# q and k turned into high and low parts, the attention scores as three part products, and one turn moved behind two score blocks

## The chip, the cores and the metric

The kernel runs on one core of a Trainium2 chip. The metric is the device time of one execution in microseconds (us): for the kernel before, the median of three runs. TensorE (PE) multiplies matrices out of the on-chip memory into eight accumulation banks of 128 x 512 fp32; PEld in the profile is its loading of the stationary operand. VectorE (DVE) and ScalarE (ACT) read the banks and do the elementwise work, and SyncE (SP) issues nearly all transfers.

## The reference, cut to what matters

One decoder layer on x of 256 x 1024 in fp32. Two attention branches of 8 heads of 64 work side by side on the same normalised input: "MoBA" (branch 0, with a rotary embedding on 16 of the 64 dimensions; at 256 positions there is one block, so it is causal attention) and "FoX" (branch 1, with a forget gate's cumulated logarithm added to the scores).

```python
h = rms_norm(x, attn_norm_g)
qa, ka, va, qb, kb, vb, f_logit, g_logit = split(h @ w_in)
qa, ka = partial_rope(rms_norm(qa, gq_a)), partial_rope(rms_norm(ka, gk_a))
qb, kb = rms_norm(qb, gq_b), rms_norm(kb, gk_b)
o_a = softmax(causal(qa @ ka.T / 8)) @ va                      # 8 heads
o_b = softmax(causal(qb @ kb.T / 8 + c[t] - c[s])) @ vb        # c = cumsum(log_sigmoid(f))
gates = sigmoid(g_logit + b_gate)
x = x + (gates[0] * (o_a @ w_moba) + gates[1] * (o_b @ w_fox)) @ w_out
u, g = split(rms_norm(x, ffn_norm_g) @ w_ffn_up)
x = x + (silu(conv3(g)) * u) @ w_ffn_down
```

## The kernel before, in words

All 256 positions stay on the chip; S = 256 is two tiles of P = 128 (NT = 2), and the 1024 features are KT = 8 slices. Weights stream through three raw buffers of 1 MB. Each half of such a buffer is split once: ACT rounds it into a high part (`whi`, L125, type fp32r), DVE subtracts that from the raw weights and leaves the low part (`wlo`, L126). There are six buffers of either, and `use` (L129) asks for the part five halves ahead of the one it hands out. The activations are split in the same manner (`xh`, `xl`). Every large product is then three products of parts, high x high, high x low and low x high, accumulated in one bank.

Not so the scores. `finish_qk` (L242) leaves normalised q or k of a branch in `qn`, positions on the partitions, as plain fp32. `turn_qk` (L271) transposes it on PE, block by block of 64 positions x 128 features (two heads) with an identity of 64 x 64: per branch 16 transposes for q and 16 for k, into two banks each; r says which half of the 64-row blocks and so which bank. ACT copies each of the four banks out, times the norm's gain, into `qT0`, `kT0`, `qT1`, `kT1` (L282), which hold two heads on 128 partitions: an even head on partitions 0 to 63, an odd one on 64 to 127. `scores(br, pair)` (L364) takes two heads: for each query tile t and head j one plain fp32 product (L374) of q's 128 positions with the first (t + 1) x 128 keys, 128 or 256 columns, out of 64 partitions; head j has a bank of its own. DVE then adds the mask or the bias and takes the row's extreme in one operation (L379, two per head: 128 and 256 columns), ACT takes the exponential and its sum (L382), DVE inverts (L384) and scales (L387). `turn` (L390) transposes the probabilities and `values` (L403) multiplies them by V. `gate` (L440) is a product of parts for the gates: of 256 columns, three per slice (L436 to L438), from a bank that DVE scales away (L443).

The order of PE's work is the program's order: it is written out by hand (`manual_schedule`, L48, and the list from L453 on). The order on ACT and DVE is made by a planner when the kernel is built; it can put an operation that is ready ahead of an earlier one that is not. The eight banks of the accumulation memory are handed out by one pool (`bank`, L53), so who gets a bank waits for the last reader of the one that had it. The part of PE's list around the change:

```python
    project(5, pv, 1)
    finish_v(pv, 1)
    forget_bias()
    turn_qk(qn, kn, 1)
    scores(0, 2)
    scores(0, 3)
    gate(0)
    gate(1)
    turn(0, 2)
```

Earlier on the list, `turn_qk(qn, kn, 0)` stands in the middle of projection 3, `scores(0, 0)` and `scores(0, 1)` in the middle of projection 4 and the four `scores(1, ...)` behind gates 1 and 3. Projections are L236 in the profile.

Two small tiles matter only as space: `sqs` (L543) and `rs2` (L568) of the second norm.

Of the kernel before, what the change touches and what calls it, by code (L numbers as in the profile page):

```python
# [8 lines left out]
F32 = mybir.dt.float32  # L9
F32R = mybir.dt.float32r  # L10
BF16 = mybir.dt.bfloat16
AF = mybir.ActivationFunctionType
ALU = mybir.AluOpType
# [4 lines left out]
P = 128  # L18
S = 256
NT = 2  # L20
D = 1024
KT = D // P
HD = 64
# [13 lines left out]
C_G2, C_BG, C_CW, C_CB, C_QG, C_BF, C_GR = 0, 8, 24, 90, 112, 116, 124  # L37
# [4 lines left out]
def decoder_block(ctx, tc, a, out):  # L42
    nc = tc.nc
# [6 lines left out]
    def T(shape, tag, bufs=1, dt=F32):  # L50
        return sb.tile(shape, dt, tag=tag, bufs=bufs, name=tag)

    def bank():  # L53
        return ps.tile([P, 512], F32, tag="bank", bufs=8, name="bank")
# [9 lines left out]
    for tag in ("xh", "xl"):  # L64
        T([P, KT, S], tag, 1, F32R)
    T([P, 2, KT, S], "pp", 1, F32R)
    for tag in ("qT0", "kT0", "qT1", "kT1"):
        T([P, 4, S], tag)

    nc.scalar.preload_act_table_set("natural_log_exp_and_others")  # L70

# [66 lines left out]
    def col(c, n=1):  # L138
        return sm[:, c:c + n]
# [59 lines left out]
    def apart(ap, b=2):  # L199
        return ap.rearrange("p (b t a) -> p b a t", b=b, a=2)  # L200

    def halves(ap):
        return ap.rearrange("p b (a t) -> p b a t", a=2)

    def halfrow(row, b=2):
        return row.rearrange("p (a t) -> p a t", a=2)[:, None].to_broadcast([P, b, 2, P])
# [35 lines left out]
    def finish_qk(pt, br, isk):  # L242

        qn = T([P, NT, NH, HD], "qn", 2)
        ss = T([P, NT, NH], "ss", 2)
        for t in range(NT):
            sq = T([P, W4], "sq", 2)
            nc.scalar.activation(sq, pt[t], AF.Square, scale=rs[:, t:t + 1])
            nc.vector.tensor_reduce(ss[:, t], sq.rearrange("p (h d) -> p h d", h=NH), axis=AX.X, op=ALU.add)
        f = T([P, NT, NH], "qf", 2)  # L250
        rsqrt_mean(f.rearrange("p t h -> p (t h)"), ss.rearrange("p t h -> p (t h)"), HD, [NT * NH], "qfv")
        for t in range(NT):
            nc.vector.tensor_scalar(f[:, t], f[:, t], rs[:, t:t + 1], 1.0 if isk else -HD ** -0.5, op0=ALU.mult, op1=ALU.mult)
            nc.vector.tensor_tensor(qn[:, t], pt[t].rearrange("p (h d) -> p h d", h=NH),
                                    f[:, t, :, None].to_broadcast([P, NH, HD]), op=ALU.mult)
        if br == 0:
            rc, rsn = rope[isk]
            p1 = T([P, NT, NH, 16], "p1", 1)
            p2 = T([P, NT, NH, 16], "p2", 1)
            x16 = qn[:, :, :, 0:16]  # L260
            nc.vector.tensor_tensor(p1, x16, rc[:, :, None, :].to_broadcast([P, NT, NH, 16]), op=ALU.mult)
            nc.vector.tensor_tensor(p2, x16, rsn[:, :, None, :].to_broadcast([P, NT, NH, 16]), op=ALU.mult)
            nc.vector.tensor_tensor(qn[:, :, :, 0:8], p1[:, :, :, 0:8], p2[:, :, :, 8:16], op=ALU.add)
            nc.vector.tensor_tensor(qn[:, :, :, 8:16], p1[:, :, :, 8:16], p2[:, :, :, 0:8], op=ALU.add)
        return qn


    turned = {}
    parts = [(slice(HD * r, HD * (r + 1)), ident[HD * r:HD * (r + 1), HD * r:HD * (r + 1)]) for r in range(2)]

    def turn_qk(qn, kn, br):  # L271

        for isk, (n, tag) in enumerate(((qn, "qT"), (kn, "kT"))):
            dst = T([P, 4, S], f"{tag}{br}")
            two = banks()
            for t in range(NT):
                for b in range(4):
                    c = slice((4 * t + b) * HD, (4 * t + b + 1) * HD)
                    for r, (rows, eye) in enumerate(parts):
                        nc.tensor.transpose(two[r][:, c], n[rows, t, 2 * b:2 * b + 2].rearrange("p h d -> p (h d)"), eye)  # L280
            for r in range(2):
                nc.scalar.activation(dst.rearrange("p b (t r c) -> p r t b c", t=NT, r=2)[:, r], two[r].rearrange("p (t b c) -> p t b c", t=NT, b=4),  # L282
                                     AF.Copy, scale=col(C_QG + 2 * br + isk))
            turned[br, isk] = dst


    bias = T([P, NH, 384], "bias")
# [64 lines left out]
    def forget_bias():  # L352

        tri_mask = mask3[:, None, 0:P].to_broadcast([P, NH, P])
        nc.vector.tensor_tensor(bias[:, :, 0:P], bias[:, :, P:2 * P], tri_mask, op=ALU.add)
        nc.vector.tensor_tensor(bias[:, :, 2 * P:3 * P], bias[:, :, 2 * P:3 * P], tri_mask, op=ALU.add)
# [7 lines left out]
    def scores(br, pair):  # L364
        s = T([P, 2, 384], "s", 3)
        nm = T([P, 2, 2], "nm", 4)
        l = T([P, 2, 2], "l", 4)
        sps = banks()
        for t in range(NT):
            for j in range(2):  # L370
                dst = sps[j][:, t * P:t * P + (t + 1) * P]
                ts, us = slice(t * P, (t + 1) * P), slice(0, (t + 1) * P)
                rows = parts[j][0]
                nc.tensor.matmul(dst, turned[br, 0][rows, pair, ts], turned[br, 1][rows, pair, us], start=True, stop=True)  # L374
        for j in range(2):
            h = 2 * pair + j
            sp = sps[j]
            for i, c in enumerate((slice(0, 128), slice(128, 384))):
                nc.vector.tensor_tensor_reduce(s[:, j, c], sp[:, c], mask3[:, c] if br == 0 else bias[:, h, c],  # L379
                                               scale=1.0, scalar=3e38, op0=ALU.add, op1=ALU.min, accum_out=nm[:, j, i:i + 1])  # L380
            for i, c in enumerate((slice(0, 128), slice(128, 384))):
                last_exp[:] = [nc.scalar.activation(s[:, j, c], s[:, j, c], AF.Exp, scale=-1.0, bias=nm[:, j, i:i + 1], accum_out=l[:, j, i:i + 1])]  # L382
        r = T([P, 2, 2], "r", 4)
        nc.vector.reciprocal(r, l)  # L384
        for j in range(2):
            for i, c in enumerate((slice(0, 128), slice(128, 384))):
                nc.vector.tensor_scalar_mul(s[:, j, c], s[:, j, c], r[:, j, i:i + 1])  # L387
        probs[br, pair] = s
# [29 lines left out]
    rsB = T([P, S], "rsB")  # L418
# [7 lines left out]
    def twin(kind, c, dst, mh, ml):  # L426

        for h in range(2):
            wh, wl = use((kind, c), h)
            for i in range(2):  # L430
                o = dst[:, i * S:(i + 1) * S]
                for k4 in range(4):
                    k = 4 * h + k4
                    w = slice(k4 * 256 + i * P, k4 * 256 + (i + 1) * P)
                    rh, rl = pairs(mh[:, k]), pairs(ml[:, k])
                    nc.tensor.matmul(o, wh[:, w], rh, start=(k == 0 and i == 0), stop=False)  # L436
                    nc.tensor.matmul(o, wh[:, w], rl, start=False, stop=False)  # L437
                    nc.tensor.matmul(o, wl[:, w], rh, start=False, stop=(k == KT - 1 and i == 1))  # L438

    def gate(c):  # L440
        gp = bank()
        twin("wg", c, gp, xh, xl)
        nc.vector.tensor_tensor(halves(gates[:, c]), apart(gp), halfrow(rsB), op=ALU.mult)  # L443
# [6 lines left out]
    def banks():  # L450
        return [bank() for _ in range(NT)]
# [6 lines left out]
    qn = finish_qk(pq, 0, 0)  # L458
# [3 lines left out]
    kn = finish_qk(pk, 0, 1)  # L462
# [4 lines left out]
    pq = banks()  # L467
    project(3, pq, 0)
    turn_qk(qn, kn, 0)
    project(3, pq, 1)  # L470
    forget_c()
    qn = finish_qk(pq, 1, 0)
    pk = banks()
    project(4, pk, 0)
    forget_d()
    scores(0, 0)
    scores(0, 1)
    project(4, pk, 1)
    kn = finish_qk(pk, 1, 1)
# [4 lines left out]
    project(5, pv, 1)  # L484
    finish_v(pv, 1)
    forget_bias()
    turn_qk(qn, kn, 1)
    scores(0, 2)
    scores(0, 3)
    gate(0)  # L490
    gate(1)
    turn(0, 2)
# [25 lines left out]
    for c in range(4):  # L518
# [11 lines left out]
        for j in range(2):  # L530
            b = 2 * c + j
# [8 lines left out]
    sq2 = T([P, 4, 2 * S], "V")  # L540
    acc = [bank() for _ in range(4)]
    x1 = xT
    sqs = T([P, S], "sqs")  # L543
    for c in range(4):
        for h in range(2):
            wh, wl = use(("wo", c), h)
            j = 2 * (c % 2) + h
# [8 lines left out]
            if c >= 2:  # L556
                xx = x1[:, 2 * j:2 * j + 2]
                nc.vector.tensor_tensor(halves(xx), apart(acc[j]), halves(xx), op=ALU.add)
                for b in (2 * j, 2 * j + 1):
                    g = col(C_G2 + b)  # L560
# [4 lines left out]
    for dst, src in ((0, 1), (2, 3), (0, 2)):  # L565
        nc.vector.tensor_tensor(sq2[:, dst], sq2[:, dst], sq2[:, src], op=ALU.add)
    nc.vector.tensor_tensor(sqs, sq2[:, 0, 0:S], sq2[:, 0, S:2 * S], op=ALU.add)
    rs2 = T([P, S], "rs2")  # L568

    def norm2():  # L570
        sp = bank()
# [153 lines left out]
```

## Time and profile before

| What | Value |
|---|---|
| Median of three runs | 356.55 us (356.46 to 356.7) |
| The profiled execution | 357.34 us, of which the span from the first to the last instruction is 355.5 us |
| Mean granted clock of TensorE | 0.999 |
| HBM read and written | 66.60 MB and 1.06 MB, 190 GB/s over the span |
| Loading from HBM, share of 16 engines | 51.7% |

A row of the chain or of a timeline starts with its start in us from the span's start and its length in us; then come the engine, the line of the kernel, and what is written from what. A row of groups has the count behind an x, then the busy time in us, the mean duration of one in ns, and the idle time of the engine just before, with what ended it. A plain fp32 product that the program issues once appears as two matmul records.

### The profile page before, as it was taken

What the parts mean: (1) busy time and instruction counts of PE and PEld (TensorE: products, weight loads), DVE (VectorE), ACT (ScalarE), POOL (GpSimd) and SP (SyncE); (2) the same over time, 40 slices, a digit from 0 to 9 for tenths busy, and PEclk for the clock granted to TensorE, in tenths of its full rate; (3) what the DMA queues carried; (4) which work ended last, traced back from release to release, by engine and by line L of the source; (5) the groups of instructions that cost most, each with busy time, mean ns of one, the idle gap of its engine ahead of it and who ended that gap; (6) DMA issues with size and microseconds to landing.
All of it is one profiled execution on the core that took longest, in us unless ns stands there. A gap on an engine that the chain in (4) does not pass through costs nothing.

```text
span 355.5 us, 6596 instructions
## 1 busy us (share of the span) xinstructions
PE 350.4 (99%) x2620; PEld 324.3 (91%) x2620; DVE 285.5 (80%) x534; ACT 228.8 (64%) x406; POOL 0.4 (0%) x6
## 2 busy tenths in 40 slices
PE   8999999999999999999999999999999999999995
PEld 4888888889899999999999999999999999999995
DVE  4989969888867756994997998897878788797953
ACT  5967576678849873553878866665756656666620
POOL 0000000000000000000000000000000000000000
PEclk9999999999999999999999999999999999999999
DMA  7986663663624453545644358655645646554003
GB/s 259 410 336 237 221 255 130 227 237 120 238 92 147 133 225 118 202 166 227 229 144 187 153 165 295 211 193 206 236 162 194 238 166 205 223 189 167 2 0 118
DMA packets 12558, 68.07 MB, mean 191 GB/s; under 512 B 1512, under 2 KB 3696, under 8 KB 5104
## 3 DMA queue, kind: packets, MB, share of 16 engines
q1 hardware_dynamic: 11328, 66.60, 51.7%
q10 hardware_dynamic: 1200, 1.06, 1.0%
q8 instruction: 20, 0.33, 0.4%
q14 instruction: 10, 0.08, 0.1%
HBM read 66.60 MB, written 1.06 MB: 190 GB/s over the span
## 4 chain that ended last, share of the span: by engine, by line
PE 98%; ACT 1%; DVE 0%; issue 0%
PE bank L590 22%; PE bank L236 18%; PE bank L591 11%; PE bank L641 6%; PE bank L640 6%; PE bank L639 5%; PE bank L436 4%; PE bank L438 4%; PE bank L437 4%; PE bank L527 2%; PE bank L555 2%; PE bank L554 2%; PE bank L529 2%; PE bank L528 2%; PE bank L553 2%; PE bank L411 2%
## 5 line engine op out<-in xcount | busy, mean ns | idle before, releaser
L126 DVE TENSOR_TENSOR wlo<-raw,whi 128x1024 fp32r<-128x1024 f32 x118 | 144.0, 1222 | 38.2 <-ACT whi L125 37.2
L125 ACT ACTIVATE whi<-raw 128x1024 fp32r<-128x1024 f32 x118 | 123.7, 1054 | 66.5 <-PE bank L590 20.7
L590 PE MATMUL bank<-pp,whi 128*128 128x512 f32 x352 | 116.2, 383 | 0.0
L591 PE MATMUL bank<-pp,wlo 128*128 128x256 f32 x352 | 95.9, 273 | 0.0
L590 PEld LDWEIGHTS bank<-pp,whi 128*128 128x128 f32 x352 | 66.6, 189 | 9.2
L591 PEld LDWEIGHTS bank<-pp,wlo 128*128 128x128 f32 x352 | 67.6, 192 | 0.0
L436 PE MATMUL bank<-xh,whi 128*128 128x256 f32 x128 | 35.6, 278 | 0.1
L437 PE MATMUL bank<-xl,whi 128*128 128x256 f32 x128 | 35.2, 275 | 0.0
L438 PE MATMUL bank<-xh,wlo 128*128 128x256 f32 x128 | 35.2, 275 | 0.0
L639 PE MATMUL bank<-qT,whi 128*128 128x256 f32 x112 | 30.8, 275 | 0.0
L640 PE MATMUL bank<-qT,whi 128*128 128x256 f32 x112 | 30.8, 275 | 0.0
L641 PE MATMUL bank<-qT,wlo 128*128 128x256 f32 x112 | 30.8, 275 | 0.0
L236 PE MATMUL bank<-whi,xh 128*128 128x512 f32 x96 | 29.8, 393 | 0.0
L236 PE MATMUL bank<-wlo,xh 128*128 128x512 f32 x96 | 29.1, 385 | 0.0
L236 PE MATMUL bank<-whi,xl 128*128 128x512 f32 x96 | 28.7, 380 | 0.0
L436 PEld LDWEIGHTS bank<-xh,whi 128*128 128x128 f32 x128 | 24.6, 192 | 1.1 <-ACT qT L282 0.5
L438 PEld LDWEIGHTS bank<-xh,wlo 128*128 128x128 f32 x128 | 24.6, 192 | 0.0
L437 PEld LDWEIGHTS bank<-xl,whi 128*128 128x128 f32 x128 | 24.6, 192 | 0.0
L639 PEld LDWEIGHTS bank<-qT,whi 128*128 128x128 f32 x112 | 21.5, 192 | 0.2
L640 PEld LDWEIGHTS bank<-qT,whi 128*128 128x128 f32 x112 | 21.5, 192 | 0.0
L641 PEld LDWEIGHTS bank<-qT,wlo 128*128 128x128 f32 x112 | 21.5, 192 | 0.0
L236 PEld LDWEIGHTS bank<-wlo,xh 128*128 128x128 f32 x96 | 18.3, 192 | 3.1 <-DVE wlo L103 0.6
(158 smaller groups left out, 644.7 us busy)
## 6 DMA issues: line engine op xcount, KB each, us to landing
raw<-in_wu SPq DMA_DIRECT2D x22, 1024.0 KB, 4.8
raw<-in_wd SPq DMA_DIRECT2D x11, 1024.0 KB, 4.8
raw<-in_qkv SPq DMA_DIRECT2D x9, 1024.0 KB, 5.0
raw<-in_wg SPq DMA_DIRECT2D x8, 1024.0 KB, 4.9
raw<-in_wb SPq DMA_DIRECT2D x4, 1024.0 KB, 5.2
raw<-in_wo SPq DMA_DIRECT2D x4, 1024.0 KB, 4.8
lead<-in_lead SPq DMA_DIRECT2D x8, 384.0 KB, 6.6
raw<-in_qkv SPq DMA_DIRECT2D x2, 512.0 KB, 8.0
```

Source lines behind the costliest of these rows:

```text
L125: whi = nc.scalar.activation(hi, raw, AF.Copy)
L126: nc.vector.tensor_tensor(lo, raw, hi.bitcast(F32), op=ALU.subtract)
L236: nc.tensor.matmul(pt[t], lhs[:, k, t * P:(t + 1) * P], rhs, start=(k == 0 and i == 0), stop=(k == KT - 1 and i == 2))
L411: nc.tensor.matmul(op[o:o + HD, n * S + i * P:(n + 1) * S], V[:, i, vc:vc + HD], pT[:, j, c], start=(i == 0), stop=(i == 1))
L436: nc.tensor.matmul(o, wh[:, w], rh, start=(k == 0 and i == 0), stop=False)
L437: nc.tensor.matmul(o, wh[:, w], rl, start=False, stop=False)
L438: nc.tensor.matmul(o, wl[:, w], rh, start=False, stop=(k == KT - 1 and i == 1))
L590: nc.tensor.matmul(two[i], wh[:, w], both, start=(k == 0), stop=False)
L591: nc.tensor.matmul(two[i][:, 0:S], wl[:, w], high, start=False, stop=(k == KT - 1))
L639: nc.tensor.matmul(o, wh[:, w], ah, start=first, stop=False)
L640: nc.tensor.matmul(o, wh[:, w], al, start=False, stop=False)
L641: nc.tensor.matmul(o, wl[:, w], ah, start=False, stop=end)
```

## The change

`turn_qk` leaves q and k as a high part (ACT, rounded to fp32r, times the gain) and a low part (DVE, the bank times the gain minus the high part); the low tiles `qL` and `kL` serve both branches in turn, and the tiles' inner order becomes tile by tile of positions (t, then pair, then 128 positions). Each of the four products of a `scores` call becomes three products of parts in fp32r, issued in the order of query tile, product, head. `turn_qk(qn, kn, 1)` moves behind `scores(0, 3)`. The space for the two new tiles comes from two small ones: `sqs` lies in a free part of `sq2`, and `rs2` takes the place of `rsB`.

```diff
-    for tag in ("qT0", "kT0", "qT1", "kT1"):
-        T([P, 4, S], tag)
+    for tag in ("qT0", "kT0", "qT1", "kT1", "qL", "kL"):
+        T([P, 4, S], tag, 1, F32R)
...
         for isk, (n, tag) in enumerate(((qn, "qT"), (kn, "kT"))):
-            dst = T([P, 4, S], f"{tag}{br}")
+            hi = T([P, NT, 4, P], f"{tag}{br}", 1, F32R)
+            lo = T([P, NT, 4, P], tag[0] + "L", 1, F32R)
             two = banks()
...
             for r in range(2):
-                nc.scalar.activation(dst.rearrange("p b (t r c) -> p r t b c", t=NT, r=2)[:, r], two[r].rearrange("p (t b c) -> p t b c", t=NT, b=4),
-                                     AF.Copy, scale=col(C_QG + 2 * br + isk))
-            turned[br, isk] = dst
+                h, l = (x.rearrange("p t b (r c) -> p r (t b) c", r=2)[:, r] for x in (hi, lo))
+                src = two[r].rearrange("p (n c) -> p n c", c=HD)
+                g = col(C_QG + 2 * br + isk)
+                nc.scalar.activation(h, src, AF.Copy, scale=g)
+                nc.vector.scalar_tensor_tensor(l, src, g, h.bitcast(F32), op0=ALU.mult, op1=ALU.subtract)
+            turned[br, isk] = hi, lo
...
         sps = banks()
+        todo = {}
         for t in range(NT):
             for j in range(2):
                 dst = sps[j][:, t * P:t * P + (t + 1) * P]
-                ts, us = slice(t * P, (t + 1) * P), slice(0, (t + 1) * P)
                 rows = parts[j][0]
-                nc.tensor.matmul(dst, turned[br, 0][rows, pair, ts], turned[br, 1][rows, pair, us], start=True, stop=True)
+                (qh, ql), (kh, kl) = turned[br, 0], turned[br, 1]
+                for i, (lhs, rhs) in enumerate(((qh, kh), (qh, kl), (ql, kh))):
+                    todo[t, i, j] = (dst.rearrange("p (u c) -> p u c", c=P), lhs[rows, t, pair], rhs[rows, 0:t + 1, pair])
+        for t, i, j in sorted(todo):
+            nc.tensor.matmul(*todo[t, i, j], start=(i == 0), stop=(i == 2))
...
-    turn_qk(qn, kn, 1)
     scores(0, 2)
     scores(0, 3)
+    turn_qk(qn, kn, 1)
     gate(0)
...
-    sqs = T([P, S], "sqs")
+    sqs = sq2[:, 1, 0:S]
...
-    rs2 = T([P, S], "rs2")
+    rs2 = T([P, S], "rsB")
```

## The prediction

> **What bounds the kernel now.** I read the page's busy table first, then the chain that ended last.
>
> ```profile
> span 355.5 us, 6596 instructions
> ...
> PE 350.4 (99%) x2620; PEld 324.3 (91%) x2620; DVE 285.5 (80%) x534; ACT 228.8 (64%) x406; POOL 0.4 (0%) x6
> ...
> PE 98%; ACT 1%; DVE 0%; issue 0%
> ```
>
> TensorE (PE) is busy for 99% of the span and is 98% of the chain; VectorE (DVE) and ScalarE (ACT) matter only where PE waits for them. So the question is what the change does to PE's own time around the scores, and whether it makes or ends a wait. The chain in order of time, its longest pieces, shows the scores (L374) and the one piece in these stages that is not PE:
>
> ```profile
> 58.22 1.51 PE bank L374 x16
> ...
> 76.38 1.27 ACT V L240 x2
> 77.65 0.94 ACT whi L125
> 78.59 0.59 ACT qT L282
> 79.22 0.38 PE bank L436
> ...
> 91.10 1.37 PE bank L374 x16
> ...
> 107.02 1.37 PE bank L374 x16
> ```
>
> Each row is a block of two calls of `scores`; the fourth lies between 76 and 79 us, where the chain leaves PE: gate 0 (L436) starts at 79.22, when ACT's first copy of q's turned bank (L282) ends. PE's timeline there:
>
> ```profile
> 75.96 0.59 PE L236 MATMUL bank<-whi,xl 128*128 128x512 f32 x2
> 76.49 1.22 PE L280 MATMUL bank<-cst,qn 64*128 64x64 f32 x32
> 77.55 1.53 PE L374 MATMUL bank<-kT,qT 64*128 64x128 f32 x16
> 79.22 0.38 PE L436 MATMUL bank<-xh,whi 128*128 128x256 f32 x1
> 79.44 0.28 PE L437 MATMUL bank<-xl,whi 128*128 128x256 f32 x1
> 79.55 0.28 PE L438 MATMUL bank<-xh,wlo 128*128 128x256 f32 x1
> 79.66 0.28 PE L436 MATMUL bank<-xh,whi 128*128 128x256 f32 x1
> ```
>
> **The price of a score.** Durations of matmuls overlap, so I use the distance from start to start.
>
> ```profile
> L374 PE MATMUL bank<-kT,qT 64*128 64x256 f32 x32 | 4.8, 377 | 0.0
> L374 PE MATMUL bank<-kT,qT 64*128 64x128 f32 x32 | 3.4, 288 | 0.0
> L280 PE MATMUL bank<-cst,qn 64*128 64x64 f32 x64 | 2.4, 226 | 0.0
> L345 PE MATMUL bank<-cst,cc 128*8 128x128 f32 x2 | 0.4, 273 | 0.0
> L236 PE MATMUL bank<-whi,xl 128*128 128x512 f32 x96 | 28.7, 380 | 0.0
> ...
> 57.84 0.38 PE L345 MATMUL bank<-cst,cc 128*8 128x128 f32 x2
> ```
>
> L345 is one plain fp32 product (a transpose by identity on all 128 rows, with only 8 weight columns): it is two records whose starts lie 0.38 − 0.273 = 0.107 us apart for 128 columns. L236 is a product of high and low parts: two products of 512 columns start 0.59 − 0.38 = 0.21 us apart (75.96 above), one record each. So a column costs 0.41 ns in the part format, and a plain fp32 product passes its columns twice in each of two records: four passes against one. That is what the change hopes to use: three single passes for four.
>
> But the heads already run side by side. Per call of `scores` there are 64 / 8 = 8 records, four of 128 columns (0.107 us each) and four of 256 (0.214 us). One after another that is 1.28 us per call, 2.57 us for two; the block takes 1.37 us. So the two heads, on rows 0 to 63 and 64 to 127, share the time: 2 x 0.107 + 2 x 0.214 = 0.64 us per call, 1.28 us per block, and the other 0.09 us is the entry and the exit. "Side by side" adds nothing.
>
> And the new form is held by weight loads. The loads (PEld):
>
> ```profile
> L436 PEld LDWEIGHTS bank<-xh,whi 128*128 128x128 f32 x128 | 24.6, 192 | 1.1 <-ACT qT L282 0.5 <-ACT pT L400 0.3 <-issue 0.2
> L374 PEld LDWEIGHTS bank<-kT,qT 64*128 64x128 f32 x64 | 4.5, 188 | 0.4 <-issue 0.2
> L280 PEld LDWEIGHTS bank<-cst,qn 64*128 64x128 f32 x64 | 2.2, 140 | 0.7 <-issue 0.7
> L345 PEld LDWEIGHTS bank<-cst,cc 128*8 128x8 f32 x2 | 0.2, 86 | 0.2
> ```
>
> 8 columns take 86 ns and 128 columns 188 ns: 102 ns for 120 columns, 0.85 ns a column, so 128 columns occupy the load path for 0.109 us, and the part format is no quicker (192). Every product loads its weights again, even the same ones (L436 and L437 both use whi). Of a chain of such products each step then takes the larger of its passes and a load: with 256 columns 0.105 against 0.109, seen as 0.11 between 79.44, 79.55 and 79.66; with 128 columns 0.053 against 0.109. After the change a call is six steps (three products by two query tiles) of two heads at a time. The low price of a step is 0.111 us, as L436 to L438 show. The high one is 0.115: in the transposes of L280 two heads' steps are (1.22 − 0.226) / 15 = 0.066 us apart, while their load occupies about 0.109 − (0.188 − 0.140) = 0.061, so a pair adds 0.005 to its load. A call thus goes from 0.64 us (0.65 with the step of 0.109 that a load sets on the narrow ones) to 6 x 0.111 = 0.67 or 6 x 0.115 = 0.69. The narrow tile loses what the wide one gains. Over eight calls that is (0.02 to 0.04) x 8 = +0.15 to +0.3 us; I take +0.2, nearer the upper row because the transposes are pairs too.
>
> The Trainium skill, "TensorE: Matmul & The Clock Gate", section "Back-to-back issue gap", gives about 81 ns for a 128-column product in a stream of load and product. By it, as an estimate, the three narrow steps of a call would take 0.243 us and the eight calls 0.7 us less than I forecast. The same page's Part 3 says that a load overlaps a running matmul only in another row group; by that the six steps would each pay load and passes in turn. The trace contradicts this second rule: products on all rows step at 0.11 us (79.44 to 79.66), no more than a load.
>
> **The moved turn.** Before, from the end of the last projection (75.96 + 2 x 0.215 = 76.39) to gate 0 at 79.22 are 2.83 us: turn, two calls, and the wait for ACT. After, the two calls come first, and they need only q and k of the first branch, long turned; the turn follows, without a DMA in it, passing two calls on PE's hand-written order and, on ACT and DVE, whatever the planner puts there. PE then has: change to 64 rows 0.10 (76.39 to 76.49), first exposed load 0.10, twelve steps of 0.111 to 0.115 = 1.33 to 1.38, sixteen transposed pairs at 0.066 = 1.05, change back 0.10: 2.68 to 2.73, gate 0 at 79.07 to 79.12. That is 0.10 to 0.15 us sooner, the scores' extra included. Before, gate 0 had the first of the turn's banks, as its wait for L282 shows; the banks come round in turn, the two calls and the turn have changed places, and so I expect gate 0 in the first bank of the first moved `scores`. So its wait is no more ACT's copy but DVE's reductions of that bank:
>
> ```profile
> 76.51 1.21 DVE L126 TENSOR_TENSOR wlo<-raw,whi 128x1024 fp32r<-128x1024 f32 x1
> 78.62 1.22 DVE L126 TENSOR_TENSOR wlo<-raw,whi 128x1024 fp32r<-128x1024 f32 x1 [0.91 <-ACT whi L125]
> 79.77 0.28 DVE L379 CUSTOM_DVE_ANT_0 s<-bank,cst 128x128 f32<-128x128 f32 x1
> ...
> 80.32 0.29 DVE L379 CUSTOM_DVE_ANT_0 s<-bank,cst 128x128 f32<-128x128 f32 x1
> ```
>
> The first call's scores are complete at about 76.6 + 0.68 = 77.3; DVE is in a wlo until 77.72 and then idle for 0.91. The reductions of one bank take 80.32 − 79.77 = 0.55 (the 128 and the 256 columns), so the bank is free at about 78.3, 0.8 us before PE wants it. What is late next is then PE itself.
>
> **DVE's new work.** Four subtractions per turn, eight in all, each 128x512 out of a bank:
>
> ```profile
> L254 DVE TENSOR_TENSOR qn<-bank,qf 128x512 f32<-128x512 f32 x4 | 2.6, 681 | 0.0
> ...
> 50.69 1.23 DVE L126 TENSOR_TENSOR wlo<-raw,whi 128x1024 fp32r<-128x1024 f32 x1 [1.78 <-ACT whi L125]
> ...
> 52.58 0.68 PE L236 MATMUL bank<-whi,xh 128*128 128x512 f32 x2
> ...
> 82.88 1.01 DVE L387 TENSOR_SCALAR s<-s,r 128x128 f32<-128x128 f32 x4
> ...
> 90.14 0.96 PE L398 MATMUL bank<-cst,s 64*128 64x64 f32 x24
> ```
>
> At 0.68 us (L254's row, an operation of the same size out of a bank) that is 2.7 us a turn, 5.4 us in all, counted at nothing. In the first turn the idle 1.78 us ahead of 50.69 and the rest up to 52.6 hide it; a turn's bank now comes free only after ACT's copy and DVE's subtraction, and the next projection may want one at 52.58. In the second the cover is longer: the probabilities that PE turns at 90.14 are scaled from 82.88, so 83.9 + 2.7 = 86.6 still leaves 3.5 us. If the cover were gone, PE would wait for the part that sticks out, up to 1 us in the first turn. ACT's copies keep their size. The removed tiles (sqs inside sq2, rs2 in rsB's place) add no instruction, and their first uses stay in the order of the same engine; nothing for them.
>
> **The sum.** Second block with its turn −0.10 to −0.15; the three other blocks 3 x 2 x (0.02 to 0.04) = +0.1 to +0.2; DVE 0. Together −0.05 to +0.1, about nothing. The profiled execution took 357.34 us, 0.8 above the median of the three timed runs, 356.55; on the median I forecast 356.5. A difference of 0.2%, 0.7 us, is about what can be told from none.
>
> **The rivals.** *Narrow products are not held by the load.* If the 128-column steps ran at the transposes' 0.066 us, a call would be 3 x 0.066 + 3 x 0.113 = 0.54 us, and eight calls 8 x (0.68 − 0.54) = 1.1 us below my sum: 355.4. For it: transposed pairs do run at 0.066. Against: their load is the short one (140 ns), the scores' is 188. The skill's 81 ns would lie between.
>
> *DVE holds gate 0's bank* (the other side). Its place is 76.5 to 80 us: if the planner again puts the second wlo ahead of the reductions, as it did at 78.62, they start at 79.77 and the bank is free at 80.32; gate 0 starts 80.4 rather than 79.1: 356.5 + 1.3 = 357.8. It decides from the point where DVE begins that bank after 78.5. For it: that very order in the trace. Against: there the scores came 1 us later than they will now, and the whi that this wlo needs is ready only at 78.59.
>
> *Narrow part products take the slow form.* The trace has no product of parts below 256 columns. If these ran as plain fp32, two records of two passes, a narrow step would be 0.214 and a call 3 x 0.214 + 3 x 0.113 = 0.98: +0.3 x 8 = 2.4 us, 358.9. Against: all the products of parts that are shown, of 256 and of 512 columns, pass each column once, and no row shows a format that changes its passes with the width. If the heads fell apart into twelve steps, a call would be 1.36 us and the time 362; against it stand the fp32 blocks, which share.
>
> **How the numbers follow.** My forecast 0.62, all of it within 0.2%. Narrow products fast 0.16, of which nearly all falls below 0.2%, with a little from the wait at gate 0 that ends. DVE at gate 0 0.10, the slow form 0.06, heads apart 0.02, another wait of DVE's 0.04; of these some of the last stays within 0.2%. So faster 0.17, same 0.62, slower 0.21. The forecast's own range is 356.2 to 356.9; the range that leaves out the slow form and the split heads runs from the fast narrow products, 355.3, to DVE at gate 0, 357.8.
>
> **What would show it.** Right: L374 has 96 records of one pass; two-call blocks of 1.39 to 1.47 us in the chain in place of 1.37; starts of narrow and wide steps alike 0.11 apart; L436 after the moved turn at about 79.1 with no ACT piece before it; DVE 5.4 us busier with no PE wait on it. Wrong: blocks near 1.1 us (narrow steps at 0.066), blocks near 2 us, or a DVE piece ahead of gate 0.

## The result, and the profile after

The changed kernel takes 360.66 us (median of 4 runs, 360.51 to 360.72) against 356.6 us (356.46 to 356.7) for the kernel before on the same chip: ratio 1.011, 95% interval 1.0095 to 1.0125. It is 4 us slower, where 356.5 was forecast and 357.8 was the end of the range. The profiled execution took 360.51 us with a granted clock of 0.995.

The page after, the lines that answer to those of before:

```profile
span 358.7 us, 6674 instructions
...
PE 352.3 (98%) x2652; PEld 326.2 (91%) x2652; DVE 290.3 (81%) x542; ACT 229.4 (64%) x406; POOL 0.4 (0%) x6
...
PE 95%; DMA 2%; DVE 1%; ACT 0%; issue 0%; DVEq 0%
```

PE is no longer 98% of the chain: 2% is a transfer and 1% DVE. DVE is 4.8 us busier (290.3 − 285.5) by the eight subtractions: e9 below, which has the three products without them, shows 285.4. The chain after, in order of time:

```profile
58.62 1.23 DVE wlo L126
60.09 0.35 ACT s L390
60.44 8.52 DMA bias<-cd
68.98 1.23 DVE bias L359
...
71.32 0.29 DVE s L395
71.75 0.97 PE bank L406 x12
72.71 7.06 PE bank L236 x24
79.78 1.57 PE bank L382 x24
81.35 1.00 PE bank L281 x32
82.35 0.31 PE bank L444
...
94.16 1.43 PE bank L382 x24
...
110.15 1.44 PE bank L382 x20
```

Read from below: the two last blocks of scores (L382) are 1.43 and 1.44 us, and gate 0 (L444) follows the moved turn (L281) with no ACT piece between them, both as forecast. But from 58.6 to 72.7 us the chain leaves PE. The 1 MB transfer of the forget gate's bias lands at 68.98, DVE's addition (L359) waits for it, the scaling of the second pair's probabilities (L395) stands behind that addition in DVE's queue, and PE waits for the scaling with `turn(0, 1)` (L406). None of these instructions is one that the change touches. PE's table of waits after has one row for these stages (us in total, times, the longest):

```profile
PE bank L406 <- DVE s L395: 1.4, 1, 1.4
```

DVE itself waits 5.77 us for the bias, as its timeline in the next section shows; before it was 1.76.

Where PE's time went, from the start of a step's first matmul to the start of the next step's in PE's timeline, in us (each to within 0.01):

| Step | before | after | e1 (below) |
|---|---|---|---|
| scores(0,0), (0,1) | 1.51 | 1.57 | 1.57 |
| turn(0,0), (0,1) | 0.89 | 2.88 | 0.89 |
| second half of projection 5 | 5.38 | 7.06 | 5.38 |
| q's and k's second turn with scores(0,2), (0,3) | 2.73 | 2.58 | 2.58 |
| turn(0,2), (0,3), scores(1,0), (1,1) | 2.26 | 2.32 | 2.32 |
| turn(1,0), (1,1), scores(1,2), (1,3) | 2.26 | 2.33 | 2.32 |
| sum | 15.03 | 18.74 | 15.06 |

The sum grows by 3.71 us; the spans differ by 358.7 − 355.5 = 3.2, since the first score began 0.52 us sooner in the profiled execution after (57.63 against 58.15). Of the 3.71 us, 1.99 + 1.68 are in two steps that the diff doesn't touch, 0.04 in those that it does.

### The profile page after: what moved, and what is told of

It reads as the page before. It is cut to its first block, busy times and chain, and to the rows that moved or that the text cites. A ratio compares the mean times of both kernels' runs of the same rounds, so it can differ in the third digit from the quotient of the medians.

```text
span 358.7 us, 6674 instructions
## 1 busy us (share of the span) xinstructions
PE 352.3 (98%) x2652; PEld 326.2 (91%) x2652; DVE 290.3 (81%) x542; ACT 229.4 (64%) x406; POOL 0.4 (0%) x6
## 4 chain that ended last, share of the span: by engine, by line
PE 95%; DMA 2%; DVE 1%; ACT 0%; issue 0%; DVEq 0%
PE bank L598 21%; PE bank L236 15%; PE bank L599 11%; PE bank L649 5%; PE bank L647 5%; PE bank L648 5%; PE bank L444 4%; PE bank L446 4%; PE bank L445 4%; DMA bias<-cd 2%; PE bank L535 2%; PE bank L562 2%; PE bank L561 2%; PE bank L536 2%; PE bank L563 2%; PE bank L537 2%
## 5 line engine op out<-in xcount | busy, mean ns | idle before, releaser
L444 PE MATMUL bank<-xh,whi 128*128 128x256 f32 x128 | 35.6, 278 | 0.0
L444 PEld LDWEIGHTS bank<-xh,whi 128*128 128x128 f32 x128 | 24.6, 192 | 0.4 <-issue 0.2
```

## Where the late bias comes from

DVE's timeline before and after, from the first scores on (start, length; the idle time before an operation and its releaser in brackets):

```profile
59.11 0.29 DVE L379 CUSTOM_DVE_ANT_0 s<-bank,cst 128x128 f32<-128x128 f32 x1
...
61.60 1.19 DVE L126 TENSOR_TENSOR wlo<-raw,whi 128x1024 fp32r<-128x1024 f32 x1
...
65.47 1.23 DVE L355 TENSOR_TENSOR bias<-bias,cst 128x1024 f32<-128x1024 f32 x1 [1.76 <-DMA bias<-cd]
...
67.81 1.00 DVE L387 TENSOR_SCALAR s<-s,r 128x128 f32<-128x128 f32 x4
```

```profile
58.62 1.23 DVE L126 TENSOR_TENSOR wlo<-raw,whi 128x1024 fp32r<-128x1024 f32 x1
59.76 0.28 DVE L387 CUSTOM_DVE_ANT_0 s<-bank,cst 128x128 f32<-128x128 f32 x1
...
68.98 1.23 DVE L359 TENSOR_TENSOR bias<-bias,cst 128x1024 f32<-128x1024 f32 x1 [5.77 <-DMA bias<-cd]
...
70.21 1.20 DVE L360 TENSOR_TENSOR bias<-bias,cst 128x1024 f32<-128x1024 f32 x1
71.32 1.00 DVE L395 TENSOR_SCALAR s<-s,r 128x128 f32<-128x128 f32 x4
```

The planner has put one `wlo`, that of weight half 23, ahead of the score reductions, at 58.62 instead of 61.60: 3.0 us sooner in the two profiles, 2.5 us sooner when each is counted from its first score (58.15 and 57.63). The planner also moved the second addition ahead of the scalings, from 73.48 to 70.21. The early `wlo` frees a raw buffer as much sooner, and SP, whose queue holds nothing but the next weight transfer, issues it at once. First SP's timeline, before and after (the row covers two issues; the second ends with the row), then the table of DMA issues, before for the bias alone and after for what was issued from 59.4 us on (the last number is the us from issue to landing):

```profile
55.48 7.70 SPq L121 DMA_DIRECT2D raw<-in_wg  x2
```

```profile
54.97 5.23 SPq L121 DMA_DIRECT2D raw<-in_wg  x2
```

```profile
bias<-cd ACTq DMA_DIRECT2D x1, 1024.0 KB, 5.0
```

```profile
raw<-in_wg SPq DMA_DIRECT2D x1, 1024.0 KB, 4.9
bias<-cd ACTq DMA_DIRECT2D x1, 1024.0 KB, 8.5
```

Before, the second weight issue ends at 55.48 + 7.70 = 63.18, well after the bias transfer was issued (65.4 − 5.0 = 60.4). After, it ends at 60.20, just ahead of the bias, which is issued at 60.44: two transfers of 1 MB are under way together. The weights, issued first by 0.57 us (59.87), take 4.9 us as they do alone, and the bias takes 8.5 us in place of 5.0.

The early `wlo` also holds up the issue of the bias. In ACT's queue an exponential (L390) stands between the issue of cd, the small transfer that the bias is read from, and that of the bias. It waits for DVE's first reduction, and that now stands behind the `wlo`. ACT's timeline after:

```profile
58.52 0.53 ACTq L353 DMA_DIRECT2D cd<-pT  x1
60.09 0.40 ACT L390 ACTIVATE s<-s,nm 128x128 f32<-128x128 f32 x1 [1.50 <-DVE nm L387]
60.44 0.40 ACTq L354 DMA_DIRECT2D bias<-cd  x1
```

The bias is issued 1.92 us behind cd; before it was 1.39 (59.04 to 60.43), and in e2 below, whose `wlo` is back in its place, 1.33. Without these 0.5 us the bias would have been issued at about 59.9, at the same moment as the weights. No run separates this delay from the earlier weight transfer.

The theory (Q in the expectations, where other letters stand for rivals): an early `wlo` starts a weight transfer next to the bias transfer; the bias is late, and in DVE's queue the scalings that PE waits for stand behind it. Three rivals: the new products or subtractions cost the time themselves; DVE's order alone, the additions ahead of the scalings, does it without the transfer; the halved clock that follows PE's wait makes most of it.

## The experiments

Each is compared with the kernel before on the same chip, where its median was 357.1 to 357.2 us.

**e1: the additions behind the scalings.** After, with both bias additions ordered behind the last scaling of `scores(0, 1)`:

```diff
-        nc.vector.tensor_tensor(bias[:, :, 0:P], bias[:, :, P:2 * P], tri_mask, op=ALU.add)
+        after(nc.vector.tensor_tensor(bias[:, :, 0:P], bias[:, :, P:2 * P], tri_mask, op=ALU.add), scaled[0, 1])
...
-                nc.vector.tensor_scalar_mul(s[:, j, c], s[:, j, c], r[:, j, i:i + 1])
+                scaled[br, pair] = nc.vector.tensor_scalar_mul(s[:, j, c], s[:, j, c], r[:, j, i:i + 1])
```

> The changed kernel with one more rule for DVE's order: both additions of the mask to the bias come behind the last scaling of the second pair's probabilities. Theory Q (queue): the changed kernel lost its time because DVE stood at the first of these additions for the bias transfer with the scalings queued behind it, PE then waited 1.4 us for a scaling and lost half its clock for some 3.5 us. It expects no PE wait in the second transposition of probabilities, a granted clock of 1.00 between 69 and 80 us, and 356.4 to 357.0 us (0.2 for the scores, 0.1 back from the moved turn, on 356.6). Theory P (parts): three products and eight subtractions cost the time themselves, and the wait is only where it shows. It expects 359 us or more.

Measured: 357.17 us against 357.19, ratio 1.0003 (0.9995 to 1.0012). The bias transfer is still slow (8.2 us), but nothing that PE wants stands behind it: no wait of PE's is left from 56 to 84 us. The chain there:

```profile
76.13 1.58 PE bank L383 x24
77.71 1.00 PE bank L281 x32
78.71 0.31 PE bank L445
```

All the products, subtractions and the moved turn are in this kernel. So the whole loss is the place of the two additions in DVE's queue, given the late bias; the new work itself costs nothing that can be measured.

**e2: the wlo behind the reductions.** After, with half 23's `wlo` put where it was before; the additions stay ahead of the scalings:

```diff
-            nc.vector.tensor_tensor(lo, raw, hi.bitcast(F32), op=ALU.subtract)
+            wlo = nc.vector.tensor_tensor(lo, raw, hi.bitcast(F32), op=ALU.subtract)
+            if 2 * i + h == 23:
+                after(wlo, reduced[0, 1, 1, 1])
```

> The changed kernel with another rule: the low part of weight half 23, which the planner had put ahead of the score reductions, comes behind them, as in the kernel before. The two additions to the bias stay ahead of the second pair's scalings. Theory Q says that the earlier low part freed a raw buffer 3 us sooner, so that a 1 MB weight transfer started just ahead of the 1 MB bias transfer and held it up from 5.0 to 8.5 us. It expects the bias to land at about 65.5 us again, no PE wait, 356.4 to 357.0 us. Rival O (order alone: two additions ahead of the scalings are enough): the wait stays over 1 us, 359 or more. Theory P: 359 or more.

Measured: 357.12 us, ratio 0.9998 (0.9988 to 1.0007). DVE's wait for the bias:

```profile
DVE bias L362 <- DMA bias<-cd: 1.7, 1, 1.7
```

So DVE's order of additions and scalings alone doesn't make the loss; with the bias on time it is free.

**e3: the loss without the change.** The kernel before, with nothing but that `wlo` put ahead of the first reduction:

```diff
+                if (br, pair, j, i) == (0, 0, 0, 0):
+                    after(reduced[0, 0, 0, 0], reduced[23])
...
+    load(23)
     scores(0, 0)
```

> The kernel before, plain fp32 scores and no subtractions, with the low part of weight half 23 put ahead of the score reductions. Theory Q expects the whole loss without any of the change: weight transfer ahead of the bias transfer, landing at about 69 us, a PE wait of 1 to 1.5 us and then half clock, 359.5 to 361 us. Theory P expects 356.6 us.

Measured: 360.31 us (five runs: 358.42, 358.56, 360.31, 360.7, 360.92), ratio 1.0082 (1.0056 to 1.0107). The planner then put the second addition ahead of the scalings too, as in the kernel after; e2 shows that this place alone is free. The profile is of the run of 358.56, in which the bias took 7.5 us and PE waited 0.3 us for a scaling and 0.9 us at the turn of q and k. That is less than the wait of 1.4 us in the kernel after. The times fall in two groups, and the next profile is of the other one:

> The same kernel as e3_before_wlo_ahead, for one more profile, since its times fell in two groups (358.4 to 358.6, and 360.3 to 360.9) and only one execution of the lower group has been seen. If the groups come from how long the two transfers take together, a profile near 360.5 shows the bias landing near 69 (8.5 us) with a PE wait near 1.4 us; one near 358.5 shows 67.5 (7.5 us) with 0.3 and 0.9 us of PE waits.

It is of a run of 360.74 us. PE's wait in it:

```profile
PE bank L401 <- DVE s L390: 1.3, 1, 1.3
```

The bias took 8.5 us, DVE waited 5.7 us for it, and PE's steps are those of the kernel after: 2.90 and 7.06 us for the turn and the projection half (after: 2.88 and 7.06). So the two groups go with how long the two transfers take together, as far as one profile of each can tell, and the kernel before, with one `wlo` moved, loses 3.5 us (360.74 against the 357.2 beside it) of the changed one's 4.1.

**e11: the order of the transfers alone.** After, with cd and bias issued on SP's queue ahead of the weight transfer that the early `wlo` sets free. The early `wlo` and the additions ahead of the second pair's scalings are held in their places (`forget_bias()` is called behind `scores(0, 0)` for that); of DVE's order only one reduction came to lie behind the first pair's scalings.

```diff
+                    if i == 14:
+                        after(d, fg["dma"])
...
-        nc.scalar.dma_start(cd, cT)
-        nc.scalar.dma_start(bias[:, :, P:P + S], bass.AP(tensor=cd.tensor, offset=cd.offset, ap=[[0, P], [S, NH], [1, S]]))
+        nc.sync.dma_start(cd, cT)
+        fg["dma"] = nc.sync.dma_start(bias[:, :, P:P + S], bass.AP(tensor=cd.tensor, offset=cd.offset, ap=[[0, P], [S, NH], [1, S]]))
...
+                if (br, pair) == (0, 1):
+                    after(scaled, fg["added"])
```

> The changed kernel with its orders on TensorE, VectorE and ScalarE as they are (weight half 23's subtraction ahead of the first reductions, both bias additions ahead of the second pair's scalings). Only the transfers are put in another order: cd and bias are issued on SyncE's queue, ahead of the weight transfer that the early subtraction sets free. If the two 1 MB transfers under way together are what delays the bias (8.5 us instead of 5.0): the bias lands about 65.5 to 66, the wait of the first addition is 1.8 to 2.5 us in place of 5.8, TensorE waits less than 0.2 us at the turned probabilities, and the time is that of the kernel before, within 0.2% (356.6 to 357.8). If VectorE's order alone (the bias additions queued ahead of the scalings, the subtraction ahead of the reductions) makes the loss, the time stays near 360.4 (ratio 1.008 to 1.011).

Measured: 357.05 us against 357.2, ratio 0.9996 (0.9987 to 1.0005). SP's timeline, and the landings of what was issued from 60.4 us on:

```profile
60.51 0.40 SPq L358 DMA_DIRECT2D bias<-cd  x1
61.00 0.53 SPq L121 DMA_DIRECT2D raw<-in_wg  x1
```

```profile
bias<-cd SPq DMA_DIRECT2D x1, 1024.0 KB, 4.9
raw<-in_wg SPq DMA_DIRECT2D x1, 1024.0 KB, 8.3
```

The two transfers still overlap, but now the weights take the 8.3 us and the bias 4.9. DVE's wait for it is 0.5 us (1.8 to 2.5 were expected, but DVE now comes later to the addition) and PE's none. This settles the first half of the theory: the loss hangs on which of the two transfers goes first. e11 changed the order and the queue together; that the order is enough with two queues is shown by e2, where the bias was issued 2.25 us ahead of the weights and took 5.0 us.

**e8, e5, e9: which part of the change turns the planner's order.** e8 is the changed kernel with the subtractions, the new layout and the moved turn, but with one plain fp32 product per score; e5 is the kernel before with the turn moved and nothing else; e9 is the changed kernel without the subtractions, with the product of the high parts taken three times.

```diff
-                for i, (lhs, rhs) in enumerate(((qh, kh), (qh, kl), (ql, kh))):
+                for i, (lhs, rhs) in enumerate(((qh, kh), (qh, kh), (qh, kh))):
```

> The changed kernel with its new layout, its eight subtractions and the moved turn, but with plain fp32 scores of one product; the low parts are written and not used. If the subtractions' 5.4 us on DVE have no cover (theory P's half), 1 us or more above the kernel before. If they are hidden, within 0.3 us of it, and by the moved turn rather 0.1 below.

Measured: 356.95 us, ratio 0.9992 (0.9984 to 1.0001). The planner's order is that of before (first reduction at 59.23, the `wlo` at 61.71); the eight subtractions are hidden.

> The kernel before with only the turn of q and k of the second branch moved behind the two score calls. Gate 0 no longer waits for ACT's copy: the stretch from the end of the projection to gate 0 shrinks from 2.83 us to about 2.6, so 0.1 to 0.3 us below the kernel before, which the timing can hardly tell from nothing. If DVE holds the bank of gate 0, up to 1.3 us above.

Measured: 356.9 us, ratio 0.9995 (0.9985 to 1.0005). From the second half of projection 5 to gate 0 PE takes 2.51 us (1.41 + 1.10) in place of 2.73, so the move does end the wait for ACT; a gain of 0.2 us is too small for this measurement to tell from nothing.

> The changed kernel without the eight subtractions; each score is three times the product of the high parts, so the scores are three times too large and the low parts are left out. DVE has 5.4 us less to do, and the planner still puts the low part of weight half 23 ahead of the score reductions. Theory Q expects the loss all the same, 3 to 4.3 us above the kernel before, with a PE wait of 1 us or more ahead of the second transposition of probabilities. If the subtractions were the cause, no more than 0.5 above.

Measured: 360.08 us, ratio 1.009 (1.0074 to 1.0106). The `wlo` is early again (58.33, the first reduction at 59.47). PE's two longest waits:

```profile
PE bank L405 <- DVE s L394: 1.2, 1, 1.2
...
PE bank L443 <- DVE nm L386: 0.6, 1, 0.6
```

So it is the three products, with their part format, that turn the order, not the subtractions. How the planner weighs them isn't in the profile; that it does it by the later time at which it expects the scores is only argued.

**e4 and e4b: the halved clock.** After PE's wait of 1.4 us the granted clock of the changed kernel falls. Its windows (PE, PEld, DVE, ACT, POOL busy, then clock, DMA share, GB/s):

```profile
69.00:72.50 3.50, 2.10 (x28) 1.46 (x26) 3.50 (x8) 1.06 (x1) 0.00 (x0) 1.00 0.00 0
72.50:76.20 3.70, 3.70 (x13) 2.92 (x14) 3.70 (x6) 0.30 (x2) 0.00 (x0) 0.54 0.00 0
76.20:82.30 6.10, 6.10 (x74) 5.33 (x72) 6.00 (x17) 5.18 (x12) 0.00 (x0) 1.00 0.79 318
```

The table above puts 1.68 of the 3.71 us in that projection half. To see whether the clock takes them, e4 puts 13 products of 256 columns that nothing reads into the wait:

```diff
     turn(0, 0)
+    fill = bank()
+    for n in range(13):
+        nc.tensor.matmul(fill[:, 0:S], xh[:, 0, 0:P], xh[:, 1], start=True, stop=True)
     turn(0, 1)
```

> The changed kernel with 13 products of 256 columns, whose results nobody reads, between the first and the second transposition of probabilities, that is 13 x 0.11 = 1.43 us of work where PE waits 1.4 us. If the granted clock falls because PE stands still (theory Q's second half), it now stays at 1.00 and about 3.5 us at half clock, so 1.7 us, come back: 358.7 to 359.3 us. If the slow products behind the wait have another cause, the time stays at 360.4 to 361.

Measured: 365.33 us, ratio 1.0238 (1.0216 to 1.026). This missed for a reason of its own: the extra bank shifts who gets which bank, `turn(0, 1)` got one that ACT had still to copy out, and PE waited 4.1 us for that, with the clock falling after it (0.72 from 76.2 to 82.3). It tells nothing of the question. e4b takes the fill into a bank of `turn(0, 1)`'s own:

```diff
         two = banks()
+        if (br, pair) == (0, 1):
+            for n in range(13):
+                nc.tensor.matmul(two[1][:, 0:S], xh[:, 0, 0:P], xh[:, 1], start=True, stop=True)
```

> The filling of PE's wait once more, this time in the bank that the second transposition of probabilities itself will use, so that no bank changes hands: 13 products of 256 columns ahead of it, 1.43 us where PE waits 1.4 us. If standing still is what costs the clock, the clock stays at 1.00 between 72 and 76 us and about 1.7 us come back: 1.8 to 2.4 us above the kernel before, in place of about 4. If the clock falls for another reason, 3.5 to 4.2 above.

Measured: 360.7 us, ratio 1.0102 (1.0089 to 1.0115), which can't be told from the 1.011 (1.0095 to 1.0125) of the kernel after. Its windows, and PE's waits:

```profile
69.00:72.50 3.50, 3.50 (x38) 2.91 (x36) 3.25 (x7) 1.06 (x1) 0.00 (x0) 1.00 0.00 0
72.50:76.20 3.70, 3.70 (x23) 3.13 (x22) 3.70 (x7) 0.04 (x1) 0.00 (x0) 1.00 0.00 0
76.20:82.30 6.10, 5.22 (x67) 4.22 (x66) 6.00 (x17) 5.29 (x13) 0.00 (x0) 1.00 0.84 320
```

```profile
PE bank L447 <- DVE nm L387: 0.6, 1, 0.6
PE bank L281 <- DVE qn L254: 0.3, 1, 0.3
```

The clock stays at 1.00, and turn and projection half together take 8.41 us in place of 9.94: 1.53 us less. But the scores and the turn behind them then take 4.03 in place of 2.58, 1.45 us more, with waits for DVE. In both kernels DVE is busy without a break of note from 69 to 82.3 us: 3.50 + 3.70 + 6.00 = 13.20 of 13.3 us after, 12.95 in e4b. From the first score to gate 0 that leaves 24.56 us against 24.65 after (21.07 before). So what sets gate 0's time in e4b is DVE's backlog after its 5.8 us of standing still; in the kernel after the half clock nearly only fills time that PE would have waited. e9 says the same: its clock stays at 1.00 from 57.6 to 82.3 us, and it loses 3.0 us all the same. The expectation, which gave the clock a share of its own, fell.

## Why the prediction was wrong

**What held.** The price of a score: a narrow step takes 0.11 us (79.87 to 79.98), a wide one 0.12 (80.26 to 80.38), against 0.111 to 0.115 forecast for both. The second call of this block takes 0.69 us in all (80.50 to 81.19), the upper of the two forecasts. PE's timeline of the kernel after:

```profile
79.87 0.28 PE L382 MATMUL bank<-kL,qT 64*128 64x128 f32 x2
79.98 0.28 PE L382 MATMUL bank<-kT,qL 64*128 64x128 f32 x2
80.10 0.33 PE L382 MATMUL bank<-kT,qT 64*128 64x256 f32 x2
80.26 0.28 PE L382 MATMUL bank<-kL,qT 64*128 64x256 f32 x2
80.38 0.28 PE L382 MATMUL bank<-kT,qL 64*128 64x256 f32 x2
...
82.28 0.38 PE L444 MATMUL bank<-xh,whi 128*128 128x256 f32 x1
```

The three unmoved blocks with their turns cost 0.06 + 0.06 + 0.07 = 0.19 us more (0.1 to 0.2 forecast), the moved one with its turn 0.15 less (0.10 to 0.15 forecast). The steps of e1 in the table above bear both terms out without the late bias, and the total of about nothing is what e1 and e11 measure. The products have the fast form at 128 columns, and the heads go side by side: the two rivals at 358.9 and 362 are out, and so is the one at 355.4, since a narrow step stays at 0.11 us. Gate 0 starts with no wait (82.28, behind the turn), so "DVE holds gate 0's bank" did not happen in this kernel either. In e4b and e9, where PE came earlier, gate 0 did wait 0.6 us for a reduction of DVE's: there the wait that this rival names follows from the backlog behind the late bias.

**The step that failed** is the one that closed the sum: "DVE 0", with the first block of scores taken as bound by PE alone. In its place the runs show a wait of DVE's of 5.77 us for the bias and one of PE's of 1.40 us behind it, and two steps that the change doesn't touch grow by 1.99 + 1.68 us. The prediction had left "another wait of DVE's" a chance of 0.04, with no place and no price. It asked of DVE's new work only where the operations themselves fit, and that was right: the subtractions, a little above the 0.68 us counted, are hidden (e8). The view of the four that write `qL` in the kernel after (duration in ns, lowest, median and highest, and the first and last start):

```profile
L287 DVE SCALAR_TENSOR_TENSOR qL<-bank,sm,qT x4: 744/746/749, 47.9 to 86.4; 128x512 fp32r<-128x512 f32 x4
```

The prediction did not ask what the planner does elsewhere when the scores change. "On ACT and DVE, whatever the planner puts there" was conceded for the moved block only. It was in the unmoved first block that one `wlo` changed places with eight reductions.

The rival "DVE holds gate 0's bank" had the kind right, a `wlo` ahead of the reductions, but its place (76.5 to 80 us), its mechanism (a bank that comes free late) and its price (1.3 us) were wrong. Counted from the first score, the reductions of the first block begin 2.13 us behind it (59.76 − 57.63) in place of 0.96 (59.11 − 58.15): they are late by 1.17 us, one `wlo`. No wait of PE's comes of that directly. What counted was the other thing that a `wlo` does, freeing a raw buffer, and so starting 1 MB ahead of the bias, whose own issue the late reductions held up by 0.5 us.

What in the profile of before would have shown the danger: DVE already waited 1.76 us for the bias, and the scalings that PE needs stood behind that addition. PE needs only the first of the four: after, `turn(0, 1)` begins at 71.75, 0.43 us after the scalings begin (71.32). Before they begin at 67.81, so `turn(0, 1)` could have begun at 68.24; it begins half way through a step of 0.89 us at 70.22, at about 70.67. So there were 2.4 us of slack. Counted from the first score, the wait for the bias ends 4.0 us later (68.98 − 57.63 = 11.35 against 65.47 − 58.15 = 7.32; 3.5 of it are the longer transfer and 0.5 its later issue), which uses up the slack and leaves about 1.6 us, where PE's wait shows 1.40. A chain that was 98% PE had a second one under it by 2.4 us, and a transfer in that.

## What to carry to other kernels

When a planner orders some engines, a change of what one engine does is a change of every order near it: besides where new operations fit, look in the profile of before for a transfer with little slack, and ask which buffer would come free if two neighbours changed places, and whose transfer that would start. Work that waits for a transfer shouldn't stand in an in-order queue ahead of work that doesn't and that the bounding engine needs: the same late bias cost 3.5 to 4 us with the additions ahead of the scalings and nothing behind them (e1). And a wait or a slow clock on the bounding engine is worth only what the next wait leaves: filling it (e4b) moved the time to where the same backlog was felt next.

## What was not expected of the hardware

Of two transfers of 1 MB from two queues, issued within 0.6 us of each other, the first took 4.9 us and the later one 8.5, where 5.0 was the time of the same transfer 2.4 us ahead of the other; from one queue, 0.5 us apart, the first took 4.9 and the second 8.3. The Trainium skill, "DMA: Bandwidth & Descriptors", section "Issuing engines are not separate DMA queues", says that transfers started by different engines run on the same 16 engines and interleave; the 8.5 us agree with that as to the shared engines. But the two were not slowed alike: with two queues as with one, the transfer issued first kept the time that it takes alone. The run of e3 with the bias at 7.5 us shows a little of sharing (5.2 us for the weights).

The granted clock fell to about half for some 3 us after a wait of PE's of 1.40 us (0.54 in the window from 72.5 to 76.2), and likewise after one of 1.3 us in the second profile of e3 (0.50 from 74 to 77), but stayed at 1.00 after one of 1.2 us in e9. The Trainium skill, "TensorE: Matmul & The Clock Gate", Part 1, puts the fall behind at least one idle window of about 3.4 us, free-running. Here 1.40 us of idle time in a piece was enough, so by this trace a wait well below that length can cost the clock; no run here shows where the windows lie.
